# Stored weight halves from the opening and block 0, a third result tile of the convolution, and earlier attention loads in a hybrid decoder layer

## The chip, the cores and the metric

The kernel runs on one core of a Trainium2 chip. The metric is the time of one execution in device microseconds (us), the median of three runs; lower is better. The engines' names are those of the profile: PE (matrix multiplication), PEld (its weight load), DVE (vector), ACT (activation), POOL (GpSimd) and SP, whose queue issues nearly all DMAs.

## The reference: what is computed

One decoder layer on 2048 tokens of width 1024, in float32. The projection `h @ w_in` is split into queries, keys and values for an attention with a window of 128, and into gate z, convolution channels and step sizes for a state-space scan.

```
h = modulate(rmsnorm(x, norm1_w), shift1, scale1)
q, k, v, z, xbc, dt_raw = split(h @ w_in)
attn = sliding_window_attention(rope(q), rope(k), v, sinks)
xbc  = silu(causal_depthwise_conv(xbc, conv_w, conv_b))
y    = ssd_chunked_scan(xs, softplus(dt_raw + dt_bias), A, Bm, Cm, d_skip)
y    = rmsnorm_by_group(y * silu(z)) * ssm_norm_w
x    = x + gate1 * (concat(attn, y) @ w_out)
x    = x + gate2 * swiglu(modulate(rmsnorm(x, norm2_w), shift2, scale2))
return rmsnorm(x, final_norm_w)
```

## The kernel before, in words

The tokens are cut into four blocks of 512 (`NB`), each with four tiles of 128 (`NT`). Every float32 product is made of three matmuls (`mm3`, lines 286 to 288): each operand is split into a rounded high half and the remainder, and high times high, high times low and low times high are summed in PSUM.

**Weights.** `weight` (lines 270 to 283) gives one weight in two halves. The first time it loads the raw weight (L277, tile `raw`, a ring of 5), rounds it on ACT (L278) and subtracts on DVE (L279) into a tile `w` (a ring of 6, 2 x 528 numbers per partition). With `store` set it then writes both halves to DRAM (L282, tensors `w_q..`, `w_kv..`, `w_z..`, `w_x..`), and later calls load them from there with one DMA (L274) and no work on ACT and DVE. The stores of queries, keys/values and convolution were made in block 1, those of z in block 0.

**Stages.** `opening` loads, normalizes and projects the queries and half of the keys and values of block 0; it works through four pairs of weights (`pair_ready`, L1413 to L1424 in the rows), in an order written by hand for PE, DVE, SP and ACT. Then come, for each block: `queries`, `keys_values`, `convolved` (8 chunks of channels) and `gated` (z). `two_parts` takes queries and z in two halves of the columns; each of its 8 weights feeds 24 matmuls, each weight of `tokens` (keys and values, 4 weights, taken twice) 12.

**The convolution's chunk.** `evicted` takes a PSUM bank `d` (a ring of 4): ACT copies it to `cin` (L507) and makes `cv` (L510, tile `s`), DVE adds the bank's last term (L511), which frees the bank; ACT begins a second sum in tile `sx` (L512), DVE adds to it (L513), POOL joins both (L514). `end` applies the activation in the same `sx` tile (ACT L499, DVE L501) and stores it (L502). `sx` was a ring of 2, so L512 of a chunk waits until the store of the chunk two before it has landed.

**Side work.** Attention and scan of a block run beside the next block's projections: generators (`attentions`, `ssds`) advance by one step at each `yield`, under a ratio (`tick`). In `attentions` each tile t takes keys through L623 to L625, transposes its queries (L628), copies them (L631, L632), makes scores in two halves (L663, released by DVE L672 for the next ones), probabilities (L685 to L691), transposes them (L697) and multiplies with the values (L706). `load(t + 1)` brings keys/values (L611) and queries (L612) of the next tile from DRAM. It was called after the second half's probabilities. In `ssds` L764/L766/L767 turn and scale the scan's input through bank `st`; L778 needs that bank again.

**Order.** In the projecting part PE's order is that of the code; DVE, ACT, POOL and SP are ordered by a scheduler that simulates the program. SP issues in order: one DMA that waits holds all behind it. `staged` tiles (`so`) hold query, key/value and z results until their stores have landed, a ring of 6.

Of the kernel before, what the change touches and what calls it, by code (L numbers as in the profile page):

```python
# [45 lines left out]
def hymba_layer(ctx, tc, xT, xtok, pos, wada, wadk, vecs, rows, wq, wkv, wz, wx, wo, wgu, wd, outT):  # L46
# [11 lines left out]
    def big(tag, bufs, dt=F32, pool=sb):  # L58
        return pool.tile([P, T], dt, name=tag, tag=tag, bufs=bufs)
# [329 lines left out]
    dt_of = {}  # L389

    def staged():
        return small([P, 256], "so", 6, pool=ip)

    def rope(dst, src, heads, gt, eng=nc.gpsimd):
        s4 = src.rearrange("p (h two j) -> p h two j", two=2, j=HALF)
# [11 lines left out]
    def tokens(b, h, name, srcs, n, toks, bank_of=lambda i: dense()):  # L407
        per = 2 if n == 256 else 1
        banks = [bank_of(i) for i in range(len(toks) // per)]
        plan = [(i, t, banks[i // per][:, i % per * n:i % per * n + n]) for i, t in enumerate(toks)]  # L410
        for kp in range(KT // 2):
            whi, wlo = weight(srcs[kp], 2 * n, (name, kp), b == (0 if name[0] == "z" else 1) and toks[-1] == NT - 1)
            for e in range(2):
                k, cs = 2 * kp + e, slice(e * n, (e + 1) * n)
                for i, t, out in plan:
                    ts = slice(t * P, (t + 1) * P)
                    mm3(out, h[k][0][:, ts], h[k][1][:, ts], whi[:, cs], wlo[:, cs],
                        k == 0 and i % per == 0, k == KT - 1 and i % per == per - 1)
            if kp < KT // 2 - 1 and (per == 2 or kp % 2):
                yield  # L420
        return [(t, out) for _, t, out in plan]
# [72 lines left out]
    def convolved(b, h):  # L494
        ending = []

        def end(c, cv, o):
            with behind(mybir.EngineType.Activation):
                nc.scalar.activation(o, cv, AF.Tanh)  # L499
            with behind(mybir.EngineType.DVE):  # L500
                nc.vector.scalar_tensor_tensor(o, o, 1.0, cv, ALU.add, ALU.mult)  # L501
            nc.sync.dma_start(xs_d[b][c], o)  # L502

        def evicted(c, ps):
            cin = small([P, T + 3], "cin", 2, pool=ip)
            nc.gpsimd.tensor_copy(cin[:, 0:3], halo[:, c, :])
            nc.scalar.copy(cin[:, 3:T + 3], ps)  # L507
            nc.gpsimd.tensor_copy(halo[:, c, :], cin[:, T:T + 3])
            cv, o = big("s", 3, pool=fw), big("sx", 2, pool=ip)
            nc.scalar.activation(cv, cin[:, 0:T], AF.Identity, scale=conv_w[:, c, 0:1], bias=conv_b[:, c:c + 1])  # L510
            nc.vector.scalar_tensor_tensor(cv, ps, conv_w[:, c, 3:4], cv, ALU.mult, ALU.add)  # L511
            nc.scalar.activation(o, cin[:, 1:1 + T], AF.Copy, scale=conv_w[:, c, 1:2])  # L512
            nc.vector.scalar_tensor_tensor(o, cin[:, 2:2 + T], conv_w[:, c, 2:3], o, ALU.mult, ALU.add)  # L513
            nc.gpsimd.tensor_tensor(cv, cv, o, ALU.add)  # L514
            return c, cv, o

        for c in range(8):
            ps = dense()
            for half in range(2):
                if half:  # L520
                    if ending:
                        end(*ending.pop())
                    yield
                whi, wlo = weight(wx[c, half], T, ("x", c, half), b == 1)
                for i in range(4):
                    k = 4 * half + i
                    ws = slice(i * P, (i + 1) * P)
                    mm3(ps, whi[:, ws], wlo[:, ws], h[k][0], h[k][1], k == 0, k == KT - 1)
            with urgent():
                ending.append(evicted(c, ps))  # L530
            if c == 7:
                end(*ending.pop())
            yield
# [55 lines left out]
    def attentions(b, m):  # L589
        late = []  # L590

        def values_of(sms, slots, t):
            got = {}

            def turn(half):
                pT = m.m4().bitcast(F32).rearrange("p h t -> p (h t)").rearrange("p (b j k) -> p b j k", b=4, j=2)
                for j in range(2):
                    transposed(sms[2 * half + j], pT, len(slots), j)
                yield
                if half == 0:  # L600
                    got["out"] = m.m2()
                values(got["out"], pT, slots, half)
                if half:
                    nc.sync.dma_start(spill[b][0:4, :, t * P:(t + 1) * P].rearrange("c p t -> p c t"),
                                      got["out"].rearrange("p (c t) -> p c t", c=4))
                yield
            return turn

        def load(t):
            q, kv = m.m2(), m.m1()  # L610
            nc.sync.dma_start(kv, kv_d[b * NT + t])  # L611
            nc.sync.dma_start(q, q_d[b * NT + t])  # L612
            return q, kv

        held, nxt = None, load(0)
        yield
        for t in range(NT):
            gt, (q, kv) = b * NT + t, nxt
            slot = gt % 2
            slots = [0] if gt == 0 else [0, 1]  # L620
            mask = amask[:, P:2 * P] if gt == 0 else amask[:, (1 - slot) * P:(3 - slot) * P]
            ps = bank("am", 1)
            nc.tensor.transpose(ps[:, 0:P], kv[:, 0:P], ident)  # L623
            nc.scalar.copy(k_ring[:, 0, slot, :], ps[:, 0:P])
            nc.vector.tensor_tensor(k_ring[:, 1, slot, :], ps[:, 0:P], k_ring[:, 0, slot, :].bitcast(F32), ALU.subtract)  # L625
            ps = bank("at", 1)
            for j in range(4):
                nc.tensor.transpose(ps[:, j * P:(j + 1) * P], q[:, j * P:(j + 1) * P], ident)  # L628
            qT = m.m4()
            qhi, qlo = qT[:, 0, :], qT[:, 1, :]  # L630
            nc.scalar.activation(qhi, ps, AF.Copy, scale=0.125)  # L631
            nc.vector.scalar_tensor_tensor(qlo, ps, 0.125, qhi.bitcast(F32), ALU.mult, ALU.subtract)  # L632
            st = small([P, 4, 8], "ast", 1)
            yield
            sms = []
            for pair_of in range(2):
                sms.extend(scores(m, st, qhi, qlo, slots, mask, pair_of))
                probabilities(st, sms, slots, pair_of)
                if pair_of and t + 1 < NT:
                    nxt = load(t + 1)  # L640
                yield
                if held:
                    yield from held(pair_of)
            load_values(kv, slot)
            held = values_of(sms, slots, t)
        for half in range(2):
            yield from held(half)
# [715 lines left out]
    def opening():  # L1363
# [41 lines left out]

        def pair_ready(kp, raws):

            ds, ws, xs = (2 * kp, 2 * kp + 1), [], []
            for raw in raws:
                two = wt.tile([P, 2, 528], F32R, name="w", tag="w", bufs=SPLIT)  # L1410
                ws.append((two[:, 0, 0:raw.shape[1]], two[:, 1, 0:raw.shape[1]]))
            for i in range(2):
                nc.scalar.activation(ws[i][0], raws[i], AF.Copy)  # L1413
            for d in ds:
                x = tmp()
                nc.vector.scalar_tensor_tensor(x, x0[d], scl1[:, d:d + 1], bc, ALU.mult, ALU.mult)
                h.append(operand())
                nc.scalar.activation(h[d][0], x, AF.Identity, bias=sh1[:, d:d + 1])
                xs.append(x)
            nc.scalar.activation(ws[2][0], raws[2], AF.Copy)  # L1420
            for i, d in enumerate(ds):
                nc.vector.tensor_tensor(ws[i][1], raws[i], ws[i][0].bitcast(F32), ALU.subtract)
                nc.vector.scalar_tensor_tensor(h[d][1], xs[i], sh1[:, d:d + 1], h[d][0].bitcast(F32), ALU.add, ALU.subtract)
            last = nc.vector.tensor_tensor(ws[2][1], raws[2], ws[2][0].bitcast(F32), ALU.subtract)  # L1424
            pair_done[0] = last
            first_ws.append(ws)

        rows0, rows1 = rows_of(0, common.m4), rows_of(1, common.m4)
        nc.sync.dma_start(row, rows.broadcast_to([P, 32]))
# [12 lines left out]
        ada_products(first, line, range(8))  # L1442
        vectors(1, rows1)
        main = first_columns(h)
        pair_ready(0, raws[0])
        raws.append(fetched(1))
        rows6, rows7 = rows_of(6, common.m4), rows_of(7, common.m4)
        next(main)
        vectors(4, rows4)
        vectors(5, rows5)  # L1450
        ada_columns(line, side_bank(0), 2)
        next(main)
        pair_ready(1, raws[1])
        raws.append(fetched(2))
        next(main)
        next(main)
        pair_ready(2, raws[2])
        raws.append(fetched(3))
        next(main)
        next(main)  # L1460
        vectors(6, rows6)
# [356 lines left out]
```

## Time and profile before

| what | value |
|---|---|
| three runs | 2177.98, 2178.56 (median), 2180.01 us |
| the profiled execution | 2179.79 us, of which its span is 2177.7 us |
| PE busy | 2139.7 us, 98% of the span |
| DVE busy | 1651.1 us, 76% |
| ACT busy | 1016.5 us, 47% |
| DMA engines, main queue | 63.3% of the span |

Rows of the profile name the engine, the line in the kernel and the tiles, out<-in. Matmuls overlap, so that PE's busy share hides short waits; the waits themselves are listed by the view of waits (who waited, for whom, total us, times, longest). A row of a window gives the busy time of each engine in that stretch, with its number of instructions, the granted clock, the mean busy share of the DMA engines and the bytes they moved. Block 0's projections end and block 1's begin at about 150 us; block 1's convolution runs from about 194 to 253 us.

### The profile page before, as it was taken

What the parts mean: (1) busy time and instruction counts of PE and PEld (TensorE: products, weight loads), DVE (VectorE), ACT (ScalarE), POOL (GpSimd) and SP (SyncE); (2) the same over time, 40 slices, a digit from 0 to 9 for tenths busy, and PEclk for the clock granted to TensorE, in tenths of its full rate; (3) what the DMA queues carried; (4) which work ended last, traced back from release to release, by engine and by line L of the source; (5) the groups of instructions that cost most, each with busy time, mean ns of one, the idle gap of its engine ahead of it and who ended that gap; (6) DMA issues with size and microseconds to landing.
All of it is one profiled execution on the core that took longest, in us unless ns stands there. A gap on an engine that the chain in (4) does not pass through costs nothing.

```text
span 2177.7 us, 33314 instructions
## 1 busy us (share of the span) xinstructions
PE 2139.7 (98%) x10984; PEld 1764.9 (81%) x10984; DVE 1651.1 (76%) x3195; ACT 1016.5 (47%) x2137; POOL 553.5 (25%) x658
## 2 busy tenths in 40 slices
PE   8989999999999999999999999999999999999998
PEld 6889898879778777788888878788888888888887
DVE  6987857885778866798897678777877765886576
ACT  3675735653557454433344445433333334554441
POOL 0223433322112211243441212333333331210011
PEclk9999999999999999999999999999999999999999
DMA  7798978797998332333335778645555536778553
GB/s 269 237 341 297 353 260 312 255 342 238 360 357 313 109 97 92 121 109 124 115 94 178 248 244 293 216 155 187 166 167 179 168 112 232 239 266 278 184 161 105
DMA packets 287708, 466.76 MB, mean 214 GB/s; under 512 B 27440, under 2 KB 97072, under 8 KB 287536
## 3 DMA queue, kind: packets, MB, share of 16 engines
q1 hardware_dynamic: 286960, 464.13, 63.3%
q8 instruction: 86, 1.41, 0.3%
q14 instruction: 86, 0.70, 0.1%
q10 hardware_dynamic: 576, 0.52, 0.1%
HBM read 329.73 MB, written 134.81 MB: 213 GB/s over the span
## 4 chain that ended last, share of the span: by engine, by line
PE 79%; DVE 8%; DMA 5%; ACT 3%; issue 2%; POOL 1%; SPq 0%; DVEq 0%; ACTq 0%; POOLq 0%
PE d L1182 17%; PE d L1052 9%; PE d L1051 9%; PE d L1050 9%; PE d L286 4%; PE d L287 4%; PE d L288 4%; DMA aw<-in_wada_dram 1%; PE d L1323 1%; PE am L1050 1%; PE am L1052 1%; PE am L1051 1%; PE am L706 1%; PE sm L1052 1%; PE sm L1051 1%
## 5 line engine op out<-in xcount | busy, mean ns | idle before, releaser
L1182 PE MATMUL d<-a,w 128*128 128x512 f32 x1716 | 403.5, 396 | 2.2 <-DVE a L1164 2.2
L1182 PEld LDWEIGHTS d<-a,w 128*128 128x128 f32 x1716 | 323.2, 189 | 79.6 <-DVE a L1164 2.9
L1052 PE MATMUL d<-b,w 128*128 128x512 f32 x924 | 366.9, 399 | 0.6 <-DVE w L898 0.6
L1051 PE MATMUL d<-b,w 128*128 128x512 f32 x924 | 366.6, 397 | 0.7 <-DVE b L932 0.5
L1050 PE MATMUL d<-b,w 128*128 128x512 f32 x924 | 363.2, 397 | 0.0
L897 ACT ACTIVATE w<-s 128x512 fp32r<-128x512 f32 x176 | 111.0, 631 | 237.2 <-PE d L1052 148.2
L1051 PEld LDWEIGHTS d<-b,w 128*128 128x128 f32 x924 | 174.2, 189 | 41.7 <-DVE b L932 1.5
L1052 PEld LDWEIGHTS d<-b,w 128*128 128x128 f32 x924 | 173.8, 188 | 40.4 <-DVE w L898 1.0
L1050 PEld LDWEIGHTS d<-b,w 128*128 128x128 f32 x924 | 174.2, 189 | 38.0
L286 PE MATMUL d<-w,hl 128*128 128x256 f32 (+1 forms) x592 | 171.9, 290 | 2.7 <-DVE s L511 2.7
L287 PE MATMUL d<-w,hl 128*128 128x256 f32 (+1 forms) x592 | 166.9, 282 | 0.0
L288 PE MATMUL d<-w,hl 128*128 128x256 f32 (+1 forms) x592 | 166.8, 282 | 0.0
L1178 DVE TENSOR_TENSOR w<-raw,w 128x512 fp32r<-128x512 f32 x156 | 114.0, 739 | 43.3 <-ACT w L1177 43.0
L1104 POOL TENSOR_TENSOR t<-t 128x512 f32<-128x512 f32 x44 | 75.5, 1717 | 277.0 <-DVE t L1103 126.1
L1164 DVE TENSOR_TENSOR a<-a 128x512 fp32r<-128x512 f32 x154 | 106.2, 704 | 46.1 <-ACT a L1163 45.3
L898 DVE TENSOR_TENSOR w<-s,w 128x512 fp32r<-128x512 f32 x176 | 131.1, 746 | 6.3 <-ACT w L897 5.4
L1163 ACT ACTIVATE a<-a 128x512 fp32r<-128x512 f32 x154 | 96.1, 629 | 85.1 <-DMA a<-act_t 50.1
L296 POOL TENSOR_TENSOR acc<-acc,t 128x512 f32<-128x512 f32 x35 | 51.8, 1481 | 325.7 <-ACT t L295 312.1
L286 PE MATMUL d<-hl,w 128*128 128x512 f32 x320 | 131.6, 411 | 0.0
L288 PE MATMUL d<-hl,w 128*128 128x512 f32 x320 | 126.1, 394 | 0.0
L1177 ACT ACTIVATE w<-raw 128x512 fp32r<-128x512 f32 x156 | 90.6, 587 | 75.8 <-PE d L1182 44.3
L287 PE MATMUL d<-hl,w 128*128 128x512 f32 x320 | 125.7, 393 | 0.0
(426 smaller groups left out, 4802.6 us busy)
## 6 DMA issues: line engine op xcount, KB each, us to landing
raw<-in_wgu_dram SPq DMA_DIRECT2D x176, 256.0 KB, 3.0
act_t<-t SPq DMA_DIRECT2D x88, 256.0 KB, 2.9
a<-act_t SPq DMA_DIRECT2D x88, 256.0 KB, 4.5
act_b<-t SPq DMA_DIRECT2D x66, 256.0 KB, 2.0
a<-act_b SPq DMA_DIRECT2D x66, 256.0 KB, 4.2
aw<-in_wada_dram SPq DMA_DIRECT2D x64, 256.0 KB, 5.1
w<-w_x SPq DMA_DIRECT2D x32, 512.0 KB, 5.5
raw<-wd_s SPq DMA_DIRECT2D x64, 256.0 KB, 3.2
```

The costliest lines, as they stand in the source:

```text
L286: nc.tensor.matmul(out, ahi, bhi, start=first, stop=False)
L287: nc.tensor.matmul(out, ahi, blo, start=False, stop=False)
L288: mm3.last = nc.tensor.matmul(out, alo, bhi, start=False, stop=last)
L897: nc.scalar.activation(hi, x, AF.Copy)
L898: eng.tensor_tensor(lo, x, hi.bitcast(F32), ALU.subtract)
L1050: nc.tensor.matmul(out, ahi, bhi, start=first and k == 0, stop=False, skip_group_check=True)
L1051: nc.tensor.matmul(out, ahi, blo, start=False, stop=False, skip_group_check=True)
L1052: mm3.last = nc.tensor.matmul(out, alo, bhi, start=False, stop=k == 3, skip_group_check=True)
L1163: nc.scalar.activation(hi, raw, AF.Copy)
L1164: nc.vector.tensor_tensor(lo, raw, hi.bitcast(F32), ALU.subtract)
L1178: nc.vector.tensor_tensor(w[1], raw, w[0].bitcast(F32), ALU.subtract)
L1182: mm3.last = nc.tensor.matmul(ps, w[x][:, ws], act[k][y], start=new and k == 0 and x + y == 0, stop=k == KP - 1 and x == 1, skip_group_che ...
```

## The change

- In the opening, the split query weights of the first three of four pairs are stored to DRAM: 6 stores of 512 KB. In block 0, the 4 split key/value weights are stored (528 KB each), where before block 1's second half did so.
- Block 1 therefore loads 6 of its 8 query weights and all 8 of its key/value weights in halves (L274), without splitting them; the last pair's two query weights it splits and stores as before.
- `sx` becomes a ring of 3, `so` a ring of 5.
- `load(t + 1)` in `attentions` is called after the first half's probabilities.

```diff
     def staged():
-        return small([P, 256], "so", 6, pool=ip)
+        return small([P, 256], "so", 5, pool=ip)
...
-            whi, wlo = weight(srcs[kp], 2 * n, (name, kp), b == (0 if name[0] == "z" else 1) and toks[-1] == NT - 1)
+            whi, wlo = weight(srcs[kp], 2 * n, (name, kp), b == 0)
...
-            cv, o = big("s", 3, pool=fw), big("sx", 2, pool=ip)
+            cv, o = big("s", 3, pool=fw), big("sx", 3, pool=ip)
...
-                if pair_of and t + 1 < NT:
+                if not pair_of and t + 1 < NT:
                     nxt = load(t + 1)
...
+            def stored():
+                for part in range(2):
+                    split_d[f"q{part}", kp] = dr.tile([P, 2, T], F32, name=f"w_q{part}_{kp}")
+                    nc.sync.dma_start(split_d[f"q{part}", kp], twos[part][:, :, 0:T].bitcast(F32))
+            return stored
...
-        pair_ready(0, raws[0])
+        stored = pair_ready(0, raws[0])
         raws.append(fetched(1))
         rows6, rows7 = rows_of(6, common.m4), rows_of(7, common.m4)
+        stored()
         next(main)
...
-        pair_ready(1, raws[1])
+        stored = pair_ready(1, raws[1])
         raws.append(fetched(2))
+        stored()
...
-        pair_ready(2, raws[2])
+        stored = pair_ready(2, raws[2])
         raws.append(fetched(3))
+        stored()
```

Lines from 1411 on shift by up to 10 in the changed kernel; the lines spoken of below stand where they stood. PE's order does not change up to the end of the projecting part; the other engines' orders do.

First place: SP's queue at the end of block 0's z weights, where the queries of attention's second tile are loaded (`m2<-q1_151`, L612). `w_z1_3` is the last z weight's store, `raw<-in_wq` a raw query weight, `xs0` the convolution's result. Before:

```order
L282 DMA w_z1_3_1884<-w_1879 256x1x512
L277 DMA raw_2032<-in_wq_dram 128x512
L277 DMA raw_2073<-in_wq_dram 128x512
L502 DMA xs0_198<-sx_1392 128x512
L277 DMA raw_2141<-in_wq_dram 128x512
L282 DMA w_q0_0_1967<-w_1962 256x1x512
L277 DMA raw_2191<-in_wq_dram 128x512
L502 DMA xs0_198<-sx_1479 128x512
L612 DMA m2_1703<-q1_151 128x512
L282 DMA w_q0_1_2003<-w_1998 256x1x512
```

The same place in the changed kernel:

```order
L282 DMA w_z1_3_1908<-w_1903 256x1x512
L274 DMA w_1986<-w_q0_0_478 128x2x512
L277 DMA raw_2574<-in_wx_dram 128x512
L277 DMA raw_2603<-in_wx_dram 128x512
L612 DMA m2_1659<-q1_151 128x512
L502 DMA xs0_198<-sx_1499 128x512
L277 DMA raw_2692<-in_wx_dram 128x512
L274 DMA w_2017<-w_q0_1_590 128x2x512
L274 DMA w_2045<-w_q1_0_480 128x2x512
```

The load stood eighth behind the last z store, behind both of the convolution's last stores and a query weight's store; now it is fourth, ahead of the last convolution store. Raw convolution weights (`in_wx`) of block 1 now stand here.

Second place: SP's queue over block 1's keys and values. Before, the raw weights were all loaded by then, and their stores stand among the queries' stores (`q4_154` and so on, from the `so` tiles); this is what followed the first of them:

```order
L429 DMA q4_154<-so_2221 128x256
L429 DMA q5_155<-so_2230 128x256
L429 DMA q6_156<-so_2239 128x256
L429 DMA q7_157<-so_2248 128x256
L277 DMA raw_2616<-in_wx_dram 128x512
L282 DMA w_kv_0_2483<-w_2478 128x1056
L277 DMA raw_2645<-in_wx_dram 128x512
L429 DMA q4_154<-so_2328 128x256
L429 DMA q5_155<-so_2337 128x256
L282 DMA w_kv_1_2502<-w_2497 128x1056
```

Now:

```order
L274 DMA w_2418<-w_kv_3_956 128x1056
L429 DMA q4_154<-so_2216 128x256
L429 DMA q5_155<-so_2225 128x256
L429 DMA q6_156<-so_2234 128x256
L274 DMA w_2456<-w_kv_0_899 128x1056
L429 DMA q7_157<-so_2243 128x256
L274 DMA w_2470<-w_kv_1_918 128x1056
L429 DMA q4_154<-so_2318 128x256
L274 DMA w_2484<-w_kv_2_937 128x1056
L274 DMA w_2498<-w_kv_3_956 128x1056
L429 DMA q5_155<-so_2327 128x256
```

The second half's four loads of split weights now stand between the queries' stores, where stores of split weights stood.

Third place: DVE in block 1's convolution, around the second L767, with `w<-raw` the split of a convolution weight and `sx`, `s` the convolution's sums. Before:

```order
L341 SCALAR_TENSOR_TENSOR t_3366<-t_3366,scl1_145,bc_2852 128x512
L279 TENSOR_TENSOR w_3185<-raw_3186,w_3185 128x512
L511 SCALAR_TENSOR_TENSOR s_2950<-d_2897,vec_78,s_2950 128x512
L513 SCALAR_TENSOR_TENSOR sx_2951<-cin_2946,vec_78,sx_2951 128x512
L279 TENSOR_TENSOR w_3224<-raw_3225,w_3224 128x512
L773 TENSOR_TENSOR m1_3013<-sm_3010,upper_123 128x256
L766 TENSOR_TENSOR m2_3004<-st_2999,dtv_998 128x512
L767 TENSOR_TENSOR m2_3005<-st_2999,row_82 128x512
```

Now:

```order
L827 TENSOR_SCALAR ss_2837<-ss_2837 128x2
L279 TENSOR_TENSOR w_3143<-raw_3144,w_3143 128x512
L511 SCALAR_TENSOR_TENSOR s_2912<-d_2859,vec_78,s_2912 128x512
L766 TENSOR_TENSOR m2_2966<-st_2961,dtv_1018 128x512
L767 TENSOR_TENSOR m2_2967<-st_2961,row_82 128x512
L513 SCALAR_TENSOR_TENSOR sx_2913<-cin_2908,vec_78,sx_2913 128x512
L773 TENSOR_TENSOR m1_2975<-sm_2972,upper_123 128x256
```

L766 and L767 now follow L511 at once; the three instructions that stood between them (L513, L279, L773) come later. Around block 0's last L511, the one of chunk 7, DVE's order hardly moves: ahead of it stand 260 instructions where 263 stood, without three of 128x32 numbers (L569, L572, L573).

More of the change, by code (lines that the diff above doesn't have):

```diff
@@ L1406, in pair_ready @@
         def pair_ready(kp, raws):
-            ds, ws, xs = (2 * kp, 2 * kp + 1), [], []
+            ds, ws, xs, twos = (2 * kp, 2 * kp + 1), [], [], []
             for raw in raws:
                 two = wt.tile([P, 2, 528], F32R, name="w", tag="w", bufs=SPLIT)
+                twos.append(two)
                 ws.append((two[:, 0, 0:raw.shape[1]], two[:, 1, 0:raw.shape[1]]))
```

## The prediction

> **What bounds the kernel now.** I first read the page's totals and a table of stages (columns: stretch in us; busy time and instructions of PE, PEld, DVE, ACT, POOL; granted clock, busy share of the DMA engines, GB/s).
>
> ```profile
> PE 2139.7 (98%) x10984; PEld 1764.9 (81%) x10984; DVE 1651.1 (76%) x3195; ACT 1016.5 (47%) x2137; POOL 553.5 (25%) x658
> ...
> 36.00:118.00 82.00, 82.00 (x495) 72.32 (x494) 77.51 (x186) 53.41 (x97) 17.94 (x25) 1.00 0.75 247
> 118.00:150.00 32.00, 25.47 (x214) 23.84 (x212) 29.48 (x83) 24.88 (x71) 7.35 (x7) 1.00 0.94 335
> 150.00:194.00 44.00, 44.00 (x365) 42.55 (x366) 29.20 (x97) 20.65 (x57) 14.47 (x24) 1.00 0.82 287
> 194.00:253.00 59.00, 57.50 (x291) 45.35 (x290) 47.56 (x111) 44.22 (x105) 22.40 (x41) 1.00 0.99 357
> ```
>
> PE sets the time: 98% busy at full clock. The change removes no matmul, so it can give back only PE's idle time. Of that, 32.00 less 25.47 = 6.5 us lie at 118 to 150 us, where block 0's gate ends and block 1's queries begin, 1.5 us in block 1's convolution, and none in the opening's stage or in block 1's queries, keys and values. So the view of PE's waits between 110 and 260 us says what can be won (total us, times, longest):
>
> ```profile
> PE d L286 <- DVE s L511: 2.7, 1, 2.7
> PE at L628 <- DMA m<-q: 2.0, 1, 2.0
> PE st L778 <- DVE m L767: 1.5, 1, 1.5
> PE am L663 <- DVE ast L672: 0.7, 1, 0.7
> PE at L663 <- DVE m L632: 0.7, 2, 0.4
> PE at L663 <- DVE ast L672: 0.2, 1, 0.2
> ```
>
> Together 7.8 us. That is the ceiling of what the edits can give in the stages that they touch.
>
> **The attention loads.** The second wait is attention's second tile, whose queries were loaded late. SP's own rows and PE's:
>
> ```profile
> 132.75 0.72 SPq L282 DMA_DIRECT2D w_z<-w  x1
> ...
> 138.02 1.03 SPq L502 DMA_DIRECT2D xs<-sx  x1
> 139.09 0.55 SPq L612 DMA_DIRECT2D m<-q  x1
> ...
> 144.78 0.63 PE L628 MATMUL at<-ident,m 128*128 128x128 f32 x4 [2.04 <-DMA m<-q]
> ...
> m<-q SPq DMA_DIRECT2D x2, 256.0 KB, 4.9
> ```
>
> The load was issued at 139.09 and landed 5.7 us later; the median in this stretch is 4.9. In the new order it stands fourth behind the last z store (132.75 here), behind one load of split weights and two raw loads. At 0.72 each (0.55 to 1.03 in these rows) that puts its issue at 132.75 + 0.72 + 3 x 0.72 = 135.6, and its landing, 4.9 to 5.7 later, at 140.5 to 141.3. PE wanted it at 144.78 less 2.04 = 142.7. So the whole 2.0 us go. Some of it comes back: the scores behind it (L663) wait for DVE's L632, whose place in DVE's queue follows work on the gate that comes no sooner.
>
> ```profile
> 148.27 0.68 DVE L632 SCALAR_TENSOR_TENSOR m<-at,m 128x512 fp32r<-128x512 f32 x1
> ```
>
> L632 started at 148.27 and PE waited 0.4 us. PE now comes 2.0 us sooner. On DVE a weight split (0.7, priced below) ahead of this is gone, and ACT, which must give L631 first, has lost its half of that split; taken at the same 0.7, that is 1.4 us of the 2.0, so I give back 0.6. Net 1.4, between 0.6 and 2.0.
>
> **The third result tile.** The first wait and the third (2.7 and 1.5 us) looked like its target. The timeline shows a convolution sum held up by a store just ahead of the first:
>
> ```profile
> 125.37 0.72 ACT L512 ACTIVATE sx<-cin,vec 128x512 f32<-128x512 f32 x1 [3.17 <-DMA xs<-sx]
> 126.78 0.74 DVE L511 SCALAR_TENSOR_TENSOR s<-d,vec,s 128x512 f32<-128x512 f32 x1
> 127.58 0.39 PE L286 MATMUL d<-w,hl 128*128 128x256 f32 x1 [2.73 <-DVE s L511]
> ```
>
> ACT's 3.17 us go with a third buffer. But L512 at 125.37 belongs to the chunk whose L511 starts at 126.78, and L511 does not read `sx`: what feeds L511 had long been done, and what it waited for is its turn on DVE. DVE was full there, and full again before the third wait, at 235 us:
>
> ```profile
> 85.00:127.50 42.50, 39.84 (x200) 33.16 (x198) 42.34 (x90) 33.66 (x56) 15.46 (x18) 1.00 0.78 257
> 218.00:235.00 17.00, 15.63 (x82) 11.70 (x80) 16.86 (x26) 12.86 (x28) 6.78 (x8) 1.00 0.97 350
> ```
>
> 42.34 of 42.50 and 16.86 of 17.00 us. So the store's wait does not carry over; only the order and amount of DVE's work ahead of the releasing instruction does. For the first wait the new order has three instructions of 128x32 fewer ahead of L511 (260 for 263), at about 0.1 us each between starts: 0.3 us of the 2.7, and at most 1.3, should the different order between the last two L511 count in full (0.3, one instruction of 0.7 like the 128x512 rows here and half of another). For the wait at 235 us the new order is better by more. L513, L279 and L773 no longer stand between L511 and L766:
>
> ```profile
> 232.12 0.74 DVE L513 SCALAR_TENSOR_TENSOR sx<-cin,vec,sx 128x512 f32<-128x512 f32 x1
> 232.78 0.68 DVE L279 TENSOR_TENSOR w<-raw,w 128x512 fp32r<-128x512 f32 x1
> 233.38 0.41 DVE L773 TENSOR_TENSOR m<-sm,upper 128x256 f32<-128x256 f32 x1
> 233.72 0.68 DVE L766 TENSOR_TENSOR m<-st,dtv 128x512 f32<-128x512 f32 x1
> 234.32 0.68 DVE L767 TENSOR_TENSOR m<-st,row 128x512 f32<-128x512 f32 x1
> ```
>
> From 232.12 to 233.72 are 1.6 us, which covers the 1.5. One L501 now stands further ahead, so I take 1.2, between 0 (if L766's transposes come later than L511) and 1.5.
>
> **The stored weights.** Block 1 loses 6 query and 8 key/value splits.
>
> ```profile
> 118.00:194.00 76.00, 17.85 (x24) 1.00 0.87 307
> L279 DVE TENSOR_TENSOR w<-raw,w 128x512 fp32r<-128x512 f32 x10 | 7.3, 726 | 0.8 <-ACT w L278 0.7
> ```
>
> The first row is the splits alone: 17.85 us in 24, 0.74 us each, so 14 give DVE 10.4 us. Most of it is worth nothing, since PE is never idle from 150 to 194 us. But in 130 to 150 us five query splits stood among attention's work, and there PE waited for L672 and L632. I take 0.6 of the 0.9 us of the two L672 rows, between 0 and 0.9.
>
> The stores in the opening cost DMA time: 6 x 512 KB and 4 x 528 KB are 5.3 MB, at the 357 GB/s of the fullest stage above 14.9 us of the 82 us stage, whose DMA share rises from 0.75 to about 0.93. On SP's queue each pair's two stores wait for splits for which the raw loads behind them wait anyway (a ring of 5). PE has 82.00 busy of 82.00 there; I take nothing, and up to 2 us of loss as the bound. The shorter `so` ring I put at nothing: by the order, a tile's fifth successor comes a whole part of the weights later than its store. If a store lands late, one gate or rotation waits less than the 4.9 us of a load.
>
> **The sum.** 1.4 + 0.3 + 1.2 + 0.6 = 3.5 us. The profiled execution took 2179.79 (span 2177.7 and 2.1 around it), so it would be 2176.3; that execution lies 1.2 above the median 2178.56, which becomes 2175.1, faster by 0.16%. From 250 us to the end of the projections the order ahead of DVE's later releases is the same but for the 14 splits, so I leave the later waits alone. About 0.2%, 4.4 us, is what a measurement of this kernel can tell from no change.
>
> **Rivals.** *All six waits go* (DVE has room, and the small waits were its backlog): 7.8 us, 2170.8. For it: 10.4 us less DVE work. Against: the largest wait, 2.7 us, comes before any of the removed splits.
>
> *Nothing moves*: the terms on DVE fail and L632 takes back the load's gain, leaving 0.6: 2178.0.
>
> *Slower: the second half's split key/value loads come late.* A raw weight could be loaded far ahead into its own ring; a split one needs a free `w` tile, of which there are 6, and then goes straight to PE. SP's rows for block 2, which already loads this way, and the stretch of block 1:
>
> ```profile
> SPq L274 <- PE d L288: 25.7, 15, 3.5
> ...
> w<-w_kv SPq DMA_DIRECT2D x8, 528.0 KB, 5.1
> ...
> 180.00:194.00 14.00, 14.00 (x113) 13.34 (x112) 12.17 (x40) 5.71 (x13) 9.55 (x15) 1.00 0.74 266
> 313.00:330.00 17.00, 17.00 (x144) 16.33 (x143) 10.66 (x47) 3.95 (x13) 8.91 (x28) 1.00 0.98 362
> ```
>
> SP stood 25.7 us in 15 waits for PE to free tiles there. In block 1, 8 weights are used in 14.0 us, 1.75 each, and a load takes 5.1. Behind the queries' stores (which wait for POOL) the last four loads decide it: issued less than 5.1 us, three weights, ahead of use, each costs up to 5.1 less 1.75 = 3.4. With all four late by 2.5 us, 10 us, less the 3.5 won: 2185. Against it: block 2's stretch has the same loads and queue, and PE is busy 17.00 of 17.00.
>
> The Trainium skill, SBUF — State Buffer, Summary: rules for kernel authors, says to reckon about 358 GB/s for traffic between HBM and SBUF. By that the eight loads (4.3 MB) with the queries' stores and the mix (1.3 MB) would take an estimated 15.7 us where PE needs 14.0, 1.7 us lost, and the sum would be 1.8 instead of 3.5. The trace's 362 GB/s over block 2's stretch agrees with the figure, but PE did not wait there, since half of the loads start earlier.
>
> **How the numbers follow.** The forecast has 0.5, all waits gone 0.2, nothing 0.17, slower 0.13. The forecast's own range is 2172.5 to 2177.6 (the terms' best ends are 2.0 + 1.3 + 1.5 + 0.9 = 5.7 us, the worst 0.6 + 0.3 = 0.9). About a third of it lies beyond 4.4 us: with the rival, faster is 0.37; same is 0.51; slower 0.12. The range reaches to the all-gone case below, and above to nothing moved plus the opening's 2 us: 2170.5 to 2180.0.
>
> **What would show it.** Right: no row PE at L628 <- DMA between 110 and 260 us, the row st L778 <- DVE at 0.5 or less, the row d L286 <- DVE s L511 still above 2 us, no ACT wait of L512 for xs, 14 fewer L279. Wrong: the L511 row gone (then the store did set it), a new PE wait for w<-w_kv or w<-w_q, PE idle between 36 and 118 us, or a time above 2180.

## The result, and the profile after

The changed kernel takes 2181.9 us in the median of 12 runs (2179.26 to 2186.77), the kernel before 2178.1 in as many. The ratio is 1.0021, 95% interval 1.0013 to 1.0029: slower by 0.21%, 4.6 us (the two medians differ by 3.8), where 3.5 us less were forecast and 2180.0 was the top of the range. The profiled execution took 2182.03 us, of which its span is 2180.1.

The stages for which the prediction worked out its sum come first. The page's row of PE, then the stages with the columns of the prediction's table (granted clock, DMA share and GB/s last), and PE's waits between 110 and 260 us:

```profile
PE 2143.6 (98%) x10984; PEld 1767.1 (81%) x10984; DVE 1649.9 (76%) x3181; ACT 1006.3 (46%) x2123; POOL 569.7 (26%) x658
```

```profile
36.00:118.00 82.00, 82.00 (x495) 72.22 (x493) 77.01 (x184) 53.02 (x96) 24.21 (x25) 1.00 0.91 311
118.00:150.00 32.00, 27.27 (x223) 26.21 (x222) 29.12 (x84) 23.47 (x67) 10.17 (x8) 0.95 0.92 322
150.00:194.00 44.00, 44.00 (x363) 42.34 (x362) 23.87 (x88) 17.44 (x51) 13.93 (x27) 1.00 0.94 316
194.00:253.00 59.00, 59.00 (x308) 47.29 (x307) 52.05 (x114) 46.93 (x111) 26.75 (x39) 1.00 0.94 332
```

```profile
PE d L286 <- DVE s L511: 3.1, 1, 3.1
PE at L663 <- DVE m L632: 1.2, 1, 1.2
PE am L663 <- ACT hl L343: 0.5, 1, 0.5
```

The waits for the attention load, for L767 and for L672 are gone, the one for L511 stands, and the opening (36 to 118 us) is as busy as before with more DMA traffic. The waits together are 4.8 us instead of 7.8. Measured at the same matmul of PE's order, the changed kernel is 2.8 us ahead at 255 us and 3.8 ahead at 455 us. The new thing in these rows is a granted clock of 0.95 from 118 to 150 us, where it was 1.00.

Behind 455 us the lead is lost. The waits between 480 and 580 us, before:

```profile
PE d L287 <- DVE b L851: 1.2, 3, 0.6
PE st L778 <- DVE m L767: 0.9, 1, 0.9
PE at L628 <- DMA m<-q: 0.3, 1, 0.3
```

and in the changed kernel:

```profile
PE d L287 <- DVE b L851: 2.5, 3, 1.0
PE am L697 <- DVE ast L672: 1.3, 1, 1.3
PE st L778 <- DVE m L767: 0.6, 1, 0.6
PE at L697 <- DVE ss L827: 0.2, 1, 0.2
```

The waits grew by 2.2 us; the time lost there is 7 us. The table gives what PE needed between the same matmuls, counted in its order, with a second execution of the changed kernel (from an experiment below); the times at the left are those of before.

| from, to (us) | before | changed | changed, second |
|---|---|---|---|
| 55, 155 | 99.6 | 98.4 | 97.8 |
| 155, 255 | 100.1 | 98.4 | 98.4 |
| 255, 455 | 200.4 | 199.3 | 198.6 |
| 455, 505 | 50.0 | 53.7 | 51.3 |
| 505, 555 | 50.4 | 50.5 | 51.6 |
| 555, 605 | 50.0 | 53.5 | 52.9 |
| 605, 1303 | 697.1 | 697.7 | 697.3 |
| 1303, 1414 | 111.3 | 108.4 | 110.8 |
| 1414, 2155 | 740.9 | 741.7 | 741.6 |

Up to 455 us it gains 4.0 and 5.3 us, from 455 to 605 us it loses 7.3 and 5.4. What the rest of the loss is, PE's rows at 564 us show (start, duration, what it waited for):

```profile
564.82 0.39 PE L288 MATMUL d<-b,w 128*128 128x512 f32 x1
565.05 0.40 PE L286 MATMUL d<-b,w 128*128 128x512 f32 x1
566.48 0.51 PE L287 MATMUL d<-b,w 128*128 128x512 f32 x1 [1.03 <-DVE b L851]
...
570.21 0.63 PE L287 MATMUL d<-b,w 128*128 128x512 f32 x1
570.64 0.63 PE L288 MATMUL d<-b,w 128*128 128x512 f32 x1
```

From 564.82 to 565.05 are 0.23 us: the pace of a product of 512 columns. From 570.21 on, with nothing to wait for, it is 0.43. The granted clock of the same stretch, before and then in the changed kernel:

```profile
568.00:572.00 4.00, 4.00 (x26) 3.04 (x25) 3.71 (x12) 2.94 (x10) 1.42 (x2) 1.00 1.00 344
```

```profile
564.00:568.00 4.00, 2.32 (x6) 1.08 (x6) 4.00 (x6) 4.00 (x11) 2.17 (x2) 0.85 1.05 397
568.00:572.00 4.00, 3.23 (x8) 2.56 (x9) 2.84 (x8) 1.97 (x8) 0.16 (x1) 0.50 0.85 285
```

The clock stands at one half from 566.83 to 573.66 us, 6.83 us. All such intervals in the traces begin and end on a grid of 3.41 us. Where PE is always busy each costs half its length, 1.7 us, an estimate from 0.43 us for 0.23. Before the last 20 us of the span, where little PE work is left, the trace of before has two (at 689 and 1369 us), that of the changed kernel four (133, 492 and two at 567).

What leads to one can be counted from the starts of PE's matmuls, taking as idle what lies beyond their usual pace. In the sixteen traces of this study, from 40 to 2150 us, each of the 14 grid intervals at full clock with about 2.3 us idle or more was followed by a halved one, none with less than about 1.1 was, and between these both occur (the two bounds move by 0.1 to 0.2 us with the pace that is taken as usual). The grid does not start with the program: the same wait falls into one interval in one execution and is cut in two in another. How much of the scatter of several us between runs comes of this was not measured. The Trainium skill, TensorE: Matmul & The Clock Gate, What's actually happening, has the same grid of about 3.4 us, free-running, and the same half; it puts the fall behind a whole idle interval, and here two thirds of one were enough.

### The profile page after: what moved, and what is told of

It reads as the page before. It is cut to its first block, busy times and chain, and to the rows that moved or that the text cites. A ratio compares the mean times of both kernels' runs of the same rounds, so it can differ in the third digit from the quotient of the medians.

```text
span 2180.1 us, 33263 instructions
## 1 busy us (share of the span) xinstructions
PE 2143.6 (98%) x10984; PEld 1767.1 (81%) x10984; DVE 1649.9 (76%) x3181; ACT 1006.3 (46%) x2123; POOL 569.7 (26%) x658
## 4 chain that ended last, share of the span: by engine, by line
PE 70%; DVE 4%; DMA 2%; issue 1%; ACT 1%; POOL 0%; SPq 0%; DVEq 0%; ACTq 0%
PE d L1182 17%; PE d L1050 9%; PE d L1052 9%; PE d L1051 9%; PE d L286 3%; PE d L287 3%; PE d L288 3%; PE d L1323 1%; PE am L1050 1%; PE am L1052 1%; PE am L1051 1%; PE sm L1052 1%; PE sm L1051 1%; PE sm L1050 1%; PE am L706 1%
## 5 line engine op out<-in xcount | busy, mean ns | idle before, releaser
L296 POOL TENSOR_TENSOR acc<-acc,t 128x512 f32<-128x512 f32 x35 | 53.1, 1517 | 323.9 <-ACT t L295 314.3
```

## The experiments

All ratios are to the kernel before on the same chip, with 95% intervals. Theory: changed orders on DVE made PE wait at about 490 and 565 us, and the half clock doubled the price. Rivals: the stored weights cost the time, or the half-clock intervals fall by chance. The edits show only the parts of lines that change.

**Each part alone.** First the third result tile:

```diff
-big("sx", 2, pool=ip)
+big("sx", 3, pool=ip)
-small([P, 256], "so", 6, pool=ip)
+small([P, 256], "so", 5, pool=ip)
```

> Before with the third conv result tile alone (so ring 5). Theory (the conv tile's freedom lets L513 ahead of the split L851 at about 565 us; PE waits there, and its clock is halved for one or two stretches of 3.41 us): slower by 2 to 4 us, ratio 1.001 to 1.002, with PE rows d L287 <- DVE b L851 of about 2.5 us in sum against 1.2 before. Rival (the stored weights cost the time): no change, ratio 0.9995 to 1.0005. Third possibility (only the chance of where the 3.41 us stretches lie): no change that lasts over the rounds.

Measured: 2184.53 us, ratio 1.0036 (1.0024 to 1.0048), more than the theory's 1.002. The waits at 110 to 160 us and at 555 to 580 us:

```profile
PE d L286 <- DVE s L511: 3.8, 1, 3.8
```

```profile
PE d L287 <- DVE b L851: 2.8, 3, 1.2
```

The loss at 565 us came with this edit alone, with two half-clock intervals: from 555 to 605 us PE needed 3.6 us more than before. The wait for L511 was longer than the 2.7 us of before and followed by three half-clock intervals (129.7 to 140.0 us); 118 to 150 us took 2.0 us more. And the wait at 235 us, which the prediction put to the third tile, stands as before:

```profile
PE st L778 <- DVE m L767: 1.5, 1, 1.5
```

Next, attention's loads alone:

```diff
-                if pair_of and t + 1 < NT:
+                if not pair_of and t + 1 < NT:
```

> Before with attention's loads a step sooner alone. Theory: the 2.0 us row at L628 <- DMA m<-q is gone, L513 stays behind the splits at 565 us, so 1 to 3 us faster, ratio 0.9985 to 0.9995. Rival (what is won before 250 us is always given back at the next wait on DVE, around 490 us): no change. Rival (stored weights): no change to 2 us faster as well.

Measured: 2177.76 us, ratio 1.0006 (0.9998 to 1.0015): the gain did not come, as the rival had it. Most of it was not even won: the row at L628 is gone, but waits for L625 (1.8 us) and L699 (1.3 us) stand in its place, and in the trace the kernel is only 0.7 us ahead at 155 us and 0.3 at 255. At 490 us it then loses 3.3 us more. The waits from 480 to 510 us and the clock behind them:

```profile
PE am L697 <- DVE ast L672: 1.3, 1, 1.3
```

```profile
492.00:496.00 4.00, 3.70 (x14) 1.88 (x15) 2.55 (x12) 3.54 (x13) 2.35 (x9) 0.57 0.25 86
```

So the loss at 490 us is this edit's. Then the stored weights alone, that is the changed kernel with the other two edits taken back:

```diff
-big("sx", 3, pool=ip)
+big("sx", 2, pool=ip)
-small([P, 256], "so", 5, pool=ip)
+small([P, 256], "so", 6, pool=ip)
-                if not pair_of and t + 1 < NT:
+                if pair_of and t + 1 < NT:
```

> Before with the stored weights alone. Theory: 14 fewer splits on DVE, no change of order at 565 us, the opening unchanged (below 0.2 us there); 0 to 3 us faster, ratio 0.9985 to 1.0000. Rival (the stores and the loads of stored weights cost the time): slower by 3 to 5 us, ratio 1.0015 to 1.0025, with new PE waits for DMA or a longer stretch at 36 to 118 or 180 to 194 us.

Measured: 2180.68 us, ratio 1.0023 (1.0014 to 1.0032). The size is the rival's, the place neither's: the opening took 49.5 us between the same matmuls (55 to 105 us) as before, and the stretch from 180 to 194 us was as long as before too. One of PE's waits from 118 to 155 us, and the clock:

```profile
PE at L628 <- DMA m<-q: 3.6, 1, 3.6
```

```profile
144.00:148.00 4.00, 3.00 (x14) 3.03 (x15) 3.90 (x15) 0.94 (x2) 0.00 (x0) 0.50 1.03 347
```

With the stored weights attention's query load came later relative to PE (a wait of 3.6 us for 2.0; the load and the product meet at 145 us), and two half-clock intervals followed: 118 to 150 us took 4.6 us more than before. From 155 to 455 us the trace gains 2.9, and the wait at 235 us is gone: that gain is the stored weights', not the third tile's. The changed kernel without the third tile alone:

```diff
-big("sx", 3, pool=ip)
+big("sx", 2, pool=ip)
-small([P, 256], "so", 5, pool=ip)
+small([P, 256], "so", 6, pool=ip)
```

> The changed kernel with two conv result tiles and the so ring of 6 again: stored weights and the earlier loads alone. Theory (the third conv tile is what costs): the loss at 565 us is gone, 3 to 5 us faster than the changed kernel, so 0 to 4 us faster than before, ratio 0.998 to 1.000. Rival (stored weights cost the time): as slow as the changed kernel, ratio 1.0015 to 1.0025. Rival (what is won before 250 us is given back around 490 us whatever the conv ring): ratio 1.000 to 1.001, with a half-clock stretch near 490 us.

Measured: 2181.49 us, ratio 1.0022 (1.0014 to 1.0031). The loss at 565 us was gone (the L851 row at 1.2) and the half clock at 494 us was there, as the third possibility had it, but the time is the stored weights' rival's: the whole did not improve, and that the third tile is what costs fell. In the trace 455 to 505 us took 2.9 us more than before, and 622 to 1248 us 1.5 more, with two half-clock intervals at 692 us. Each part has its own place where it loses, and the sum of the parts is not the whole.

**Undoing one place at a time.** In the changed kernel, blocks 0 to 2 keep three result tiles and block 3 takes turns on two:

```diff
-big("sx", 3, pool=ip)
+(big("sxc", 1, pool=ip) if b < 3 and c % 3 == 2 else big("sx", 2, pool=ip))
```

> The changed kernel, but block 3's convolution takes turns on two result tiles; blocks 0 to 2 keep three. By its order L513 stands behind the splits L851 again. Theory (a changed order on DVE makes PE wait, and where PE idles over about 2 us of one 3.41 us interval its clock is halved in the next): the row d L287 <- DVE b L851 falls from 2.5 to 1.2 us and the two half-clock intervals near 567 us go; 2 to 4 us less than the changed kernel, ratio to before 1.0003 to 1.0012. Rival (half-clock intervals fall by chance, wherever): as the changed kernel, 1.0015 to 1.0025, with half-clock intervals elsewhere. Rival (the stored weights cost a fixed 4 us): 1.0015 to 1.0025 too, but with the L851 row at 1.2.

Measured: 2178.2 us, ratio 1.0006 (0.9997 to 1.0015). The waits for L851 at 565 us were 1.2 us in sum, with no half-clock interval behind them, and 555 to 605 us took 49.6 us (before 50.0, the changed kernel 53.5). The rivals, 1.0015 or more, lie at the very end of the interval; by the place they fell. Then, on top, the sooner loads in block 0 alone:

```diff
-                if not pair_of and t + 1 < NT:
+                if pair_of == (b > 0) and t + 1 < NT:
```

> As the last, and attention's loads come a step sooner in block 0 alone. By its order L208 stands behind L296 and L820 again at about 480 us. Theory: DVE's 3.1 us wait for aw falls to 2 or less, PE's row am L697 <- L672 of 1.3 us near 490 us goes with its half-clock interval; 2 to 3.5 us less than the last kernel, ratio to before 0.9990 to 1.0000. Rival (chance): 1.0015 to 1.0025. Rival (stored weights cost a fixed 4 us): 1.0010 to 1.0025.

Measured: 2176.64 us, ratio 1.0006 (0.9997 to 1.0015). L208 stands behind L296 and L820 and waits 0.6 us. Between 480 and 580 us the wait for L672 is gone, and 455 to 505 us took 50.0 us, as before, for the 52.1 of the kernel without this edit (where the wait was 1.2 us, but no half clock followed):

```profile
PE d L287 <- DVE b L851: 1.2, 3, 0.6
PE st L778 <- DVE m L767: 1.0, 1, 1.0
PE d L286 <- DVE stp L565: 0.5, 1, 0.5
```

The median fell by 1.6 us but the ratio did not, so that this step's share is not settled by the time. The same edit of the loads, on the stored weights with two tiles (the fourth kernel above):

> Two result tiles, stored weights, and the sooner loads in block 0 alone. Theory: the loss near 490 us that the kernel with all loads moved had (1.3 us of wait and a half-clock interval, 3 us) is gone: ratio to before 1.0003 to 1.0012 against the 1.0022 there. If the stored weights cost their 4 us at one place, it is the waits am L663 <- DVE L672 (2.0 us) and at L628 <- DMA m<-q at 130 to 145 us; with the load sooner the second should be below 1 us and no half-clock interval should follow it. Rival (a fixed cost of the stores in the opening or of the loads at 180 to 194 us): 1.0020 with PE later there.

Measured: 2177.6 us, ratio 1.0008 (0.9999 to 1.0017), as expected: 0.0014 less than with all loads moved, and no half-clock interval at 144 or 490 us. So the stored weights have no fixed price of 4 us; a smaller one is not excluded. And on the kernel before, with nothing else:

```diff
-                if pair_of and t + 1 < NT:
+                if pair_of == (b > 0) and t + 1 < NT:
```

> Before, with attention's loads a step sooner in block 0 alone: two result tiles, no stored weights. Theory: the 2.0 us wait at 144 us is gone and nothing is given back at 490 us; 1.5 to 3.5 us faster than before, ratio 0.9984 to 0.9993. Rival (a gain before 250 us is given back at the next wait on DVE whatever the order there): 0.9998 to 1.0006, as with all the loads moved.

Measured: 2182.03 us, ratio 1.0025 (1.0016 to 1.0034): both were wrong. Up to 622 us it was 2.8 us ahead of before; the stage from there to 1248 us took 631.5 us for 625.3. Waits at 670 to 700 and at 940 to 960 us, and the clock behind the two places:

```profile
PE d L1051 <- DVE b L932: 1.4, 2, 1.2
```

```profile
PE sm L818 <- ACT m L738: 1.2, 1, 1.2
```

```profile
684.00:688.00 4.00, 3.75 (x11) 3.12 (x12) 2.08 (x9) 2.65 (x10) 0.00 (x0) 0.50 1.02 360
...
956.00:960.00 4.00, 4.00 (x15) 3.45 (x16) 3.12 (x5) 1.83 (x6) 0.01 (x1) 0.57 0.90 243
```

In that stage the scheduler orders PE too: from 698 to 1207 us PE's order differs from that of before, and it does so in most kernels here. The trace shows three half-clock intervals, 5.1 us, in the place of the one of before. Why the order fell so stays open.

**Is it the half clock that costs?** In the changed kernel PE computes the first product of block 1's output projection eight times, each time starting the sum anew, just ahead of the waits for L851 (written out here over more than one line):

```diff
 # out_proj, ahead of mm3
+if (b, c, k) == (1, 0, 0):
+    for _ in range(7): nc.tensor.matmul(ps, whi[:, 0:P], mix[0][0], start=True, stop=True)
```

> The changed kernel with seven more products in front of the place where PE waits for L851 (about 562 us): the first product of block 1's output projection is computed eight times, each restarting the sum, so the result is unchanged; every other engine's order is unchanged, word for word. The seven take 7 x 0.23 = 1.6 us. Theory (PE's idle time above about 2 us in a 3.41 us interval halves its clock in the next, which costs 1.7 us each time): the waits for L851 fall from 2.5 us to about 1, the two half-clock intervals near 567 us go, and the kernel with more work is 2 to 4 us faster than the changed kernel (repeated beside it). Rival (the half clock is a sign of the wait and costs nothing by itself): the products fill the wait, so between the same time and 1 us slower.

The changed kernel ran beside it again:

> The changed kernel again, for a second trace and as the neighbour of the fill. Theory: ratio 1.0015 to 1.0030; the half-clock intervals near 491 and 567 us stand in this trace too, since the waits there come of the order, while those near 130 and 690 us may come or go with where the 3.41 us intervals lie. Rival (chance): the half-clock intervals near 491 and 567 us are gone and others have come.

And the same seven in the kernel before:

> Before with the same seven products at the same place: the control. There the wait for L851 is 1.2 us and no half-clock interval follows it in the trace of before. Theory: nothing to win; the 1.6 us of products take the place of at most 1.2 us of waiting: 0.4 to 1.6 us slower, ratio 1.0000 to 1.0008. Rival (more products help anywhere, for example by keeping weights in place): faster, below 0.9995.

Measured: with the fill 2178.91 us, ratio 1.0009 (1.0000 to 1.0018); the changed kernel again 2179.89, 1.0014 (1.0006 to 1.0023), just under what was expected; before with the fill 2176.86, 1.0001 (0.9991 to 1.0010), as expected, though its rival, below 0.9995, is inside the interval. Of the kernel with the fill, the row of the seven products, the wait behind them, and the stretch of the wait with its clock (1.00):

```profile
558.12 1.88 PE L870 MATMUL d<-b,w 128*128 128x512 f32 x7
```

```profile
PE d L287 <- DVE b L851: 1.3, 3, 0.7
```

```profile
562.00:566.00 4.00, 2.93 (x11) 1.54 (x9) 4.00 (x6) 3.05 (x11) 4.00 (x2) 1.00 1.05 398
```

In the traces the 24 products of this place took 7.77 us before, 11.73 and 11.08 in the changed kernel, and 9.42 with the seven (558.12 to 567.54): 1.7 to 2.3 us less for more work. In the ten kernels that leave the order at this place as in before and add no products there they took 7.74 to 7.78. The control agrees: before with the seven took the same 7.77 for 31 products, and no wait for L851 is left there. Where no half clock follows the wait, the products fit into it and win nothing. The whole time fell by 1.0 us between the medians, less than the 2 to 4 expected, and the intervals overlap: by the time alone the rival is not excluded, by the place it is. In the second trace of the changed kernel the half clock stood at 565.5 us again, but not at 491, though the wait was there (1.0 us): by the count of idle time the grid cut it into 1.2 and 1.7 us. The expectation of both places fell there.

A second fill, 20 products of 256 columns at the start of block 0's gate, ahead of the wait for L511, was added to the kernel with the first fill (also written out):

```diff
 # two_parts, ahead of mm3
+if (b, name, part, k, t) == (0, "z", 0, 0, 0):
+    for _ in range(20): nc.tensor.matmul(out, h[0][0][:, ts], whi[:, cs], start=True, stop=True)
```

> The changed kernel with both fills: seven products at 562 us and 20 at the start of block 0's gate. By its order DVE's, ACT's and SP's instructions stand as in the changed kernel but for a few dozen near 130 us. Theory: no half-clock interval at 130 and at 567 us; 2.5 to 5 us less than the changed kernel, ratio to before 0.9998 to 1.0008, below the one fill's 1.0009. Rival (the half clock only marks the waits): as the changed kernel, 1.0014 to 1.0021.

Measured: 2178.81 us, ratio 1.0010 (1.0000 to 1.0019), between the two forecasts. The wait for L511 shrank, another took its place, and two half-clock intervals stayed at 132 us; at 562 us the 24 products with the seven took 9.41 us, as with the first fill alone:

```profile
PE am L663 <- DVE k_ring L625: 1.9, 1, 1.9
PE d L286 <- DVE s L511: 0.7, 1, 0.7
```

DVE is behind there, and PE meets the next wait for it. So this run could not double the effect.

**Towards a better version.** Block 1's norm two to three steps sooner in block 0's convolution, on the kernel with three tiles in blocks 0 to 2 and the sooner loads in block 0:

```diff
-nxt = norm_ahead(1, (10, 13, 15, 19, 22))
+nxt = norm_ahead(1, (8, 11, 13, 16, 19))
```

> An attempt at a version that beats both: the kernel with three result tiles in blocks 0 to 2 and the sooner loads in block 0 alone, with block 1's norm begun two to three steps sooner in block 0's convolution (due at 8, 11, 13, 16, 19 instead of 10, 13, 15, 19, 22), so that L344 no longer stands ahead of the last L511. Theory: the wait d L286 <- DVE s L511 of 3.1 us falls to 1 or less and no half-clock interval follows it at about 130 us; 3 to 5 us less than the kernel without this, ratio to before 0.9980 to 0.9995. Rival (the order in the later stages decides, whatever is won here): 1.0000 to 1.0020.

Measured: 2180.97 us, ratio 1.0024 (1.0014 to 1.0034). The wait for L511 stayed at 2.7 us, so the edit did not do what it was for, and the stage from 622 to 1248 us took 629.4 us with a half clock at 958 us. That is the rival's place, though its 1.0020 was passed. The same kernel, without this, with the fill at block 0's gate:

> Three result tiles in blocks 0 to 2, the sooner loads in block 0 alone, and 20 needless products of 256 columns (20 x 0.12 = 2.4 us) at the start of block 0's gate, just ahead of the wait d L286 <- DVE s L511 of 3.1 us. Theory: that wait falls below 1 us, the two half-clock intervals at 129 us go (3.4 us), and the ratio to before falls from 1.0006 to 0.9990 to 1.0000. Rival (the half clock only marks the wait): 1.0003 to 1.0010, no change. Rival (the order in the stage from 700 to 1290 us, which the 20 products move too, decides): anything from 1.0000 to 1.0025 with new half-clock intervals there.

Measured: 2175.92 us, ratio 0.9997 (0.9988 to 1.0006), as the theory had it, with the rival's 1.0003 inside the interval. The wait for L511 fell to 0.7 us. It is the fastest of the study and no faster than before beyond doubt; one half-clock interval stayed at 131 us. No version was found that clearly beats both kernels.

## Why the prediction was wrong, point by point

*The attention load.* Right: the row at L628 <- DMA is gone. SP issued the load at 137.27 us, later than the 135.6 worked out, behind a load of split weights and two raw ones as read from the order:

```profile
134.80 0.61 SPq L274 DMA_DIRECT2D w<-w_q  x1
135.45 1.77 SPq L277 DMA_DIRECT2D raw<-in_wx_dram  x2
137.27 0.46 SPq L612 DMA_DIRECT2D m<-q  x1
```

The wait for L632 came to 1.2 us; 0.6 given back on top of its 0.7 was about right. In the run of this edit alone other waits took the place of the load's, and 0.7 us of gain was left at 155 us: the terms are not independent.

*The third tile and L511.* Right that the store's wait did not set L511: ACT's 3.2 us for `xs` went and the wait stayed, at 3.1 (2.5 in the second trace) for the 2.4 forecast. The wait of L778 at 235 us went whole, 1.5 for the 1.2 taken, and L766 does follow L511 sooner, but the edit that this was put to was wrong: with the third tile alone the wait stood at 1.5 us, with the stored weights alone it was gone. Of the 1.5 us that the sum puts to the third tile (0.3 at L511, 1.2 here) the run of the tile alone shows none; that the total came out is luck.

*L672 and the splits.* DVE has 14 instructions fewer (3181 for 3195). The two rows of L672 went; an ACT wait of 0.5 us and the longer L632 took their place.

*The opening and the stores.* Right: 82.00 of 82.00 us busy, DMA share 0.91 where 0.93 was worked out. The slower rival (split loads late at 180 to 194 us) did not occur, nor the loss of 1.7 us in the aside on bandwidth: PE has 44.00 busy of 44.00 us from 150 to 194.

*The sum up to 455 us.* The lead of 3.8 us there is near the 3.5 forecast, in part by luck: at 155 us it is 1.2 where the terms give 2.3, since the half-clock interval at 133 us costs some 1.7, and 1.0 us was won after 255 us, where nothing was forecast. In the second trace the gain from 55 to 455 us is 5.3. The range's own ends are loosely drawn: 5.7 us less are 2172.9, not 2172.5.

*The step that failed* is the one before the rivals: that from 250 us to the end of the projections "the order ahead of DVE's later releases is the same but for the 14 splits, so I leave the later waits alone". It was not. DVE's rows at 565 us before, then in the changed kernel, with POOL's row beside the latter:

```profile
565.09 0.68 DVE L851 TENSOR_TENSOR b<-b 128x512 fp32r<-128x512 f32 x1
565.69 0.16 DVE L681 TENSOR_SCALAR ast<-ast 128x4 f32<-128x4 f32 x1
565.76 0.68 DVE L501 SCALAR_TENSOR_TENSOR sx<-sx,s 128x512 f32<-128x512 f32 x1
```

```profile
565.01 0.74 DVE L513 SCALAR_TENSOR_TENSOR sx<-cin,vec,sx 128x512 f32<-128x512 f32 x1
...
565.74 0.69 DVE L851 TENSOR_TENSOR b<-b 128x512 fp32r<-128x512 f32 x1
566.34 1.77 DVE L501 SCALAR_TENSOR_TENSOR sx<-sx,s 128x512 f32<-128x512 f32 x1
```

```profile
565.83 1.73 POOL L514 TENSOR_TENSOR s<-s,sx 128x512 f32<-128x512 f32 x1 [3.79 <-DVE ast L681]
```

With a free third tile the scheduler lets L513 go ahead of the splits L851, which PE waits for: 0.7 us later. And POOL's L514, which reads what L513 writes, starts there too (the row names L681, which ended just after L513); beside it L501 took 1.77 us instead of 0.68: another 1.1. The Trainium skill, SBUF — State Buffer, Terms, says that DVE and GpSimd hold a pair of ports by turns for a whole instruction; L501's end, 0.5 us after L514's, agrees. So do the other traces. Of the 3134 DVE instructions of 128x512 numbers on L279, L344, L501, L513 and L851 in all sixteen, 312 took more than 0.85 us (up to 1.80), and each of these ended about 0.55 us after a POOL instruction with two operands; the 1944 that met no POOL instruction took 0.75 at most.

At 480 us the order of L208 changed; before, then changed:

```profile
483.81 0.69 DVE L296 TENSOR_TENSOR acc<-acc,t 128x512 f32<-128x512 f32 x1 [0.76 <-ACT t L295]
484.42 0.68 DVE L820 TENSOR_TENSOR m<-m,sm 128x512 f32<-128x512 f32 x1
485.66 0.75 DVE L208 CUSTOM_DVE_ANT_0 aw<-aw,csil,vec 128x512 f32<-128x512 f32 x1 [0.57 <-DMA aw<-in_wada_dram]
```

```profile
482.69 0.75 DVE L208 CUSTOM_DVE_ANT_0 aw<-aw,csil,vec 128x512 f32<-128x512 f32 x1 [3.14 <-DMA aw<-in_wada_dram]
...
483.37 0.69 DVE L296 TENSOR_TENSOR acc<-acc,t 128x512 f32<-128x512 f32 x1
```

L208 went ahead of L296 and L820 and waited 3.1 us for its load with both behind it; L672, which frees PE's bank `am` for L697, came late: PE waited 1.3 us for it. The kernels that put L208 back behind them have no such wait.

*The term that was missing* is the clock. The sum took a wait of PE at its own length. Of the 7.3 us lost from 455 to 605 us in the first trace, half-clock intervals make an estimated 1.7 + 3.4 = 5.1, the longer waits 2.2. What stays open: the two profiled executions differ by 2.2 us and the medians by 3.8, since before's was one of its slower ones. How much of the mean loss belongs to which place could only be bounded, through the two edits that undid them (1.0021 and 1.0014 with both, 1.0006 without the one at 565 us, 1.0006 without either). Why the kernel with two tiles and all loads moved, which lacks the loss at 565 us as well, stayed at 1.0022 is explained only in part, by its own losses at 494 and after 622 us.

## What to carry to other kernels

Where a scheduler orders the engines, an edit in one stage can move instructions far behind it: compare the order around every wait of the bound engine to the end of the program, not only in the edited stages, and ask of each moved instruction what it can wait for and who stands behind it. More room (a third tile, an earlier load) also gives the scheduler leave to put less urgent work first. On a PE that is nearly always busy, add up the idle time per clock interval: a wait that fills two thirds of one cost an estimated 1.7 us more than its length here, and needless products in that wait were cheaper at their place than the wait. Take each edit's term to the run of that edit alone: a sum that comes out does not show that its terms do.

## What the runs showed of the hardware that was not expected

- The granted clock of a kernel that is 98% busy falls to one half for single intervals of 3.41 us, after intervals with about 2.3 us or more idle; products of 512 columns then start every 0.43 us instead of 0.23.
- The mean granted clock of the runs falls into two groups some 0.004 apart: in the lower one the trace has 17.07 us at half clock at 11 to 28 us, in the upper no record of the clock before about 30 us. In the seven traces of the lower group PE came to the same matmul at 52.3 to 52.8 us, in the nine of the upper at 54.3 to 55.2, so that the groups are some 2 us apart before any edit counts; in the 27 runs of before that stood beside the first four experiments their means are 2175.9 and 2177.4 us. Both groups come with either kernel: 0.992 to 0.994 and 0.996 to 0.998 in these 27 runs of before, 0.991 to 0.993 and 0.995 to 0.996 in the first 12 of the changed kernel. Within the upper group the mean was 0.9970 for before (14 runs) and 0.9953 for the changed kernel (6 runs). 0.0017 of 2180 us are 3.7 us of clock, near the 4.6 lost, but not all of it is time: in the two traces 1.1 us of such a difference lies in the last 10 us, where little PE work is left.
- DVE instructions of 128x512 numbers that otherwise take 0.7 us took up to 1.80 us beside a POOL instruction with two operands, and then ended about 0.55 us after it.
- Kernels that differ in a few edits of no more work differ by up to 0.36% in time.
